# A third plain group becomes a Sevens group in both gated MLPs, and the plain weights' remainders move to accumulating DMAs

## The chip, the cores and the metric

The kernel runs on one core of a Trainium2 chip. Its time is the device time of one execution in microseconds (us). The engines named below are TensorE (PE; PEld is its weight load), VectorE (DVE), ScalarE (ACT), GpSimd (POOL) and SyncE (SP); the last two here mostly issue DMA transfers.

## The reference

A decoder trunk of two layers on 512 tokens of width 1024, all in float32. Layer 0 mixes by attention (8 forgetting heads and 8 stick-breaking heads), layer 1 by a gated short convolution. Each is followed by the gated MLP that this case is about (D_FF = 2816):

```python
def conv_ffn(h, norm_g, w_up, conv_w, w_down):
    xn = rms_norm(h, norm_g)
    u = causal_dwconv(xn @ w_up, conv_w)
    g, val = u[..., :D_FF], u[..., D_FF:]
    return (jax.nn.silu(g) * val) @ w_down

for layer in range(DEPTH):          # DEPTH = 2
    ...                             # h = h + the mixer of this layer
    h = h + conv_ffn(h, ffn_norm[layer], ffn_w_up[layer], ffn_conv[layer], ffn_w_down[layer])
```

## The kernel before

**Float32 on TensorE.** Each float32 operand is split into a rounding ("hi") and a remainder ("lo"), and a product is three matmuls: hi hi, hi lo, lo hi (`mm3`, L283 to L285). For weights, ScalarE writes the rounding `whi` (L262) and VectorE subtracts it from the raw weight to give `wlo` (L263). Weights that a `want` call asks for come in chunks of 128 x 1024 values (512 KB) by SP's queue into a tile `raw`; `fetch` runs AHEAD = 2 chunks before use, and `whi`, `wlo` and `raw` have three buffers each.

**The up projection** of an MLP makes 22 + 22 tiles of 128 columns, in 11 groups of two gate and two value tiles. The first CLASSIC groups are plain: per group 2 pairs x 2 halves x 8 k-tiles x 3 matmuls on 512 tokens. The other groups go by class `Sevens`, a scheme of seven block products instead of eight: p1, p7, p3, p6, p2, q5, q4, each of 24 matmuls on 256 tokens (`seven`, L1010). Its weights come as four 512-KB blocks X, Y, W, Z; Y and X get a second block added by accumulating POOL transfers (`add_block`, L1033), Y also takes X (L1062) and W (L1106) on VectorE. `halves_to` makes their halves (ACT L959, DVE L963 or L965). For p3 the previous group is used, so the first Sevens group ("base group") runs p1, p7, p6, p2, q5, q4.

**Chores.** The VectorE and ScalarE work beside the plain groups is written as generators: `normed` multiplies a PSUM accumulator by the row of the norm (L1201), `prepare` makes the moving operands of the Sevens (L1185, L1192, L963), `gate_one` runs the convolution (L390, L393), SiLU and the product of gate and value (L997, L998). `work_off(us)` lets that much of them be issued per three matmuls (SHARE) or per slot of the base group.

**The down projection** (L1527) is again the seven products, in the order p1, p7, p2, p6, p3, q5, q4, each in six steps of 2, 2, 2, 1, 2, 2 k-tiles. Before a step, `operand` makes the halves of its activations, `sums` updates the blocks of activations (L1428 to L1432), `bring` and the chain transfers (L236, L238) add weight blocks; for three of them a block `other` is loaded and added by VectorE into `Y_chain`, `p1_hi_chain` or `p1_lo_chain` (L233). L1463 adds a finished accumulator to the residual. Layer 0 streams activations of 256 columns, layer 1 streams weights of 512 columns.

**Order.** A tile scheduler orders the instructions of each engine by its own estimate of times. What is passed to `tc.keep_in_program_order` stays in the order in which the program emits it, against other instructions so marked on that engine. The hi parts of the Sevens' weights (L959) and the POOL transfers are so marked.

## Time and profile before

| | us |
|---|---|
| median of 3 runs | 1135.77 (1134.57 to 1136.08) |
| the profiled execution | 1138.21 |
| its span in the trace | 1136.2 |
| TensorE busy in it | 1122.1 |
| plain groups of layer 0 | 278.95 to 346.60 |
| Sevens groups of layer 0 | 346.60 to about 504 |
| down projection of layer 0 | about 504 to 600 |
| plain groups of layer 1 | 793.7 to 861.7 |
| down projection of layer 1 | about 1018 to 1132 |

The profile comes from one execution. Its page gives the busy time of each engine, the chain of work that ended last, the costliest groups of instructions and the DMA issues; further views of the same trace give the waits of an engine, its instructions in order of time, and tables of busy time by stretch. "A <- B: t" in the waits means that A sat idle until B was done. "DMA share" is the mean busy share of the core's 16 DMA engines, and the clock is the one granted to TensorE, 1.00 being full. Line numbers are those of the kernel before.

### The profile page before, as it was taken

The numbers are of one execution on the slowest core, as the hardware profiler recorded it, in microseconds if no ns is written. First come the engines' busy times: TensorE is split into PE (matmuls) and PEld (weight loads), VectorE is DVE, ScalarE is ACT, GpSimd is POOL, SyncE is SP. The second block draws the span as 40 slices with busy tenths as digits, with TensorE's granted clock in tenths as the row PEclk, the third lists the DMA queues.
The fourth block names the chain that finished last, engine by engine and source line by source line (L and its number), as shares of the span: only waits on it lengthen the run. The fifth ranks groups of instructions, "written<-read, shape, count | busy, mean of one in ns | idle before, by whom it ended". The sixth has DMA issues, their size and how long they took to land.

```text
span 1136.2 us, 19079 instructions
## 1 busy us (share of the span) xinstructions
PE 1122.1 (99%) x7547; PEld 1007.1 (89%) x7547; DVE 965.4 (85%) x1459; ACT 670.3 (59%) x999; POOL 133.0 (12%) x150
## 2 busy tenths in 40 slices
PE   8999999999999999999999999999999999999998
PEld 7888787878889999999999889988889999998886
DVE  6787888887899898989878888875798999889886
ACT  7556576755546767676547445544445766667553
POOL 4000000000012111014300001000001211014300
PEclk9999999999999999999999999999999999999999
DMA  6412212022366867689971655633375786789961
GB/s 192 112 38 75 57 39 74 26 87 75 106 182 118 191 160 163 172 235 194 224 185 31 172 118 142 130 111 93 93 195 112 167 191 137 181 220 216 230 168 56
DMA packets 160440, 155.31 MB, mean 137 GB/s; under 512 B 6396, under 2 KB 136492, under 8 KB 160352
## 3 DMA queue, kind: packets, MB, share of 16 engines
q1 hardware_dynamic: 124256, 106.94, 30.6%
q0 software_dynamic: 35936, 47.10, 25.1%
q8 instruction: 59, 0.97, 0.3%
q14 instruction: 29, 0.24, 0.1%
q10 hardware_dynamic: 160, 0.07, 0.0%
HBM read 149.10 MB, written 2.10 MB: 133 GB/s over the span
## 4 chain that ended last, share of the span: by engine, by line
PE 87%; DVE 6%; issue 2%; DMA 2%; ACT 2%; POOL 1%; DVEq 0%; SPq 0%; POOLq 0%; ACTq 0%
PE psb L1010 25%; PE psa L1010 10%; PE psb L1527 9%; PE psb L283 6%; PE psb L284 6%; PE psb L285 6%; PE psa L1527 6%; PE psa L285 4%; PE psa L283 4%; PE psa L284 4%; PE psb L658 1%; PE psa L754 1%; DMA raw<-in_ffn_w_down 1%; DVE rest L699 1%; DVE wlo L263 1%
## 5 line engine op out<-in xcount | busy, mean ns | idle before, releaser
L262 ACT ACTIVATE whi<-raw 128x1024 fp32r<-128x1024 f32 (+2 forms) x97 | 100.1, 1034 | 103.9 <-PE psb L284 31.9
L263 DVE TENSOR_TENSOR wlo<-raw,whi 128x1024 fp32r<-128x1024 f32 (+2 forms) x97 | 115.2, 1188 | 30.5 <-ACT whi L262 29.6
L1010 PE MATMUL psb<-p_hi,wlo_p 128*128 128x256 f32 x384 | 108.3, 282 | 0.6 <-DVE wlo_p L963 0.6
L1010 PE MATMUL psb<-p_lo,whi_p 128*128 128x256 f32 x384 | 108.1, 281 | 0.0
L1010 PE MATMUL psb<-p_hi,whi_p 128*128 128x256 f32 x384 | 107.8, 281 | 0.0
L283 PE MATMUL psb<-hs_a,whi 128*128 128x512 f32 x256 | 104.4, 409 | 0.0
L285 PE MATMUL psb<-hs_a,wlo 128*128 128x512 f32 x256 | 101.5, 397 | 0.0
L1010 PEld LDWEIGHTS psb<-p_hi,wlo_p 128*128 128x128 f32 x384 | 72.2, 188 | 0.8 <-DVE wlo_p L963 0.8
L1010 PEld LDWEIGHTS psb<-p_hi,whi_p 128*128 128x128 f32 x384 | 72.8, 190 | 0.0
L1010 PEld LDWEIGHTS psb<-p_lo,whi_p 128*128 128x128 f32 x384 | 72.3, 188 | 0.0
L1010 PE MATMUL psb<-q_hi,whi_q 128*128 128x256 f32 x256 | 72.0, 281 | 0.0
L1010 PE MATMUL psa<-p_lo,whi_p 128*128 128x256 f32 x256 | 72.0, 281 | 0.0
L1010 PE MATMUL psb<-q_lo,whi_q 128*128 128x256 f32 x256 | 72.0, 281 | 0.0
L1010 PE MATMUL psa<-p_hi,wlo_p 128*128 128x256 f32 x256 | 72.0, 281 | 0.0
L1010 PE MATMUL psb<-q_hi,wlo_q 128*128 128x256 f32 x256 | 72.0, 281 | 0.0
L1010 PE MATMUL psa<-p_hi,whi_p 128*128 128x256 f32 x256 | 71.8, 281 | 0.0
L1527 PE MATMUL psb<-act,whi 128*128 128x256 f32 x352 | 63.1, 282 | 0.0
L393 DVE SCALAR_TENSOR_TENSOR uv<-yv,taps,uv 128x511 f32<-128x511 f32 (+1 forms) x88 | 62.5, 744 | 0.2
L393 DVE SCALAR_TENSOR_TENSOR ug<-yg,taps,ug 128x511 f32<-128x511 f32 (+1 forms) x88 | 61.9, 743 | 0.3 <-ACT ug L390 0.3
L285 PEld LDWEIGHTS psb<-hs_a,wlo 128*128 128x128 f32 x256 | 48.1, 188 | 10.9
L283 PEld LDWEIGHTS psb<-hs_a,whi 128*128 128x128 f32 x256 | 48.4, 189 | 10.5 <-issue 1.2
L1527 PE MATMUL psb<-whi,act 128*128 128x512 f32 x176 | 56.7, 398 | 0.0
(458 smaller groups left out, 3645.7 us busy)
## 6 DMA issues: line engine op xcount, KB each, us to landing
raw<-in_attn_w_in SPq DMA_DIRECT2D x24, 512.0 KB, 4.0
raw<-in_ffn_w_up SPq DMA_DIRECT2D x24, 512.0 KB, 3.9
X<-in_ffn_w_up SPq DMA_DIRECT2D x16, 512.0 KB, 4.7
W<-in_ffn_w_up SPq DMA_DIRECT2D x16, 512.0 KB, 6.7
Y<-in_ffn_w_up SPq DMA_DIRECT2D x16, 512.0 KB, 4.5
Z<-in_ffn_w_up SPq DMA_DIRECT2D x16, 512.0 KB, 4.8
Y<-in_ffn_w_up POOLq DMA_DIRECT2D x16, 512.0 KB, 9.8
X<-in_ffn_w_up POOLq DMA_DIRECT2D x16, 512.0 KB, 7.4
```

The source lines that it names most:

```text
L262: return (act.activation(hi[:, at_], raw[:, at_], AF.Copy), dve.tensor_tensor(lo[:, at_], raw[:, at_], f32(hi[:, at_]), op=ALU.subtract))
L263: dve.tensor_tensor(lo[:, at_], raw[:, at_], f32(hi[:, at_]), op=ALU.subtract))
L283: made = [pe.matmul(acc, w[0], rhs[0], start=first, stop=False), pe.matmul(acc, w[0], rhs[1], start=False, stop=False), pe.matmul(acc, w[1 ...
L284: pe.matmul(acc, w[0], rhs[1], start=False, stop=False),
L285: pe.matmul(acc, w[1], rhs[0], start=False, stop=last)]
L393: dve.scalar_tensor_tensor(dst[:, d:], src[:, 0:S - d], tap(j), dst[:, d:], op0=ALU.mult, op1=ALU.add)
L658: pe.matmul(ss[e][:, c:c + wide], ql[rows, b * P:n], kl[rows, 0:wide], start=first and b == bs[0], stop=last and b == bs[-1])
L699: dve.tensor_tensor_scan(back, back, begin[:, S - n:S][:, ::-1], 0.0, op0=ALU.mult, op1=ALU.max)
L754: pe.matmul(out_, w, t[:, first:first + step * (NB - k - 1) + 1:step, :], start=k == 0 and i == 0, stop=k == NB - 1 and i == 1)
L1010: pe.matmul(to, w[a][:, k, c], x[b][:, k, :], start=fresh and i + k + t == 0, stop=i == 1 and k == 3 and t == 2, skip_group_check=not fresh)
L1527: pe.matmul(to, l, r, start=begin and o + t == 0, stop=end and t == 2 and o == (0 if layer else 1), skip_group_check=not fresh)
```

## The change

1. CLASSIC goes from 3 to 2 and SHARE from 0.58 to 0.68: each MLP has two plain groups and nine Sevens groups.
2. The weight chunks of the plain groups are in a set `by_dma`. For these ScalarE writes the rounding and then the negated rounding into `wlo`, and a POOL transfer adds `raw` to it; VectorE does nothing for them.
3. The accumulators of the second plain group stay in PSUM, and its `normed` and `gate_one` chores run in the slots of the first Sevens groups, at a rate that depends on the group. Their wide tiles lie in the buffer `hs_a`, which held the moving operand of the plain groups.
4. In the base group the halves for p6 are emitted ahead of a ScalarE copy.
5. In the down projections the halves of the activations (from the second phase on), the `sums` and the additions of `bring` are marked to keep the program's order.
6. The first weight chunk of the kernel is loaded in two halves.

```diff
@@ -46,8 +46,8 @@
 NSUMS, NROWS, LATE = 4.0, 3.0, 7.0
 FILL1, FILL2, BEFORE = 1.5, 3.3, 2.0
 UNITS = (0, 1), (2,), (3,)
-CLASSIC = 3
-SHARE = 0.58
+CLASSIC = 2
+SHARE = 0.68
 
 
 @with_exitstack
@@ -217,7 +217,7 @@
 
         wanted.append((place, nk, n, blocks, queue))
 
-    brought = {}
+    brought, pin = {}, tc.keep_in_program_order
 
     def bring(i):
         place, nk, n, blocks, queue = wanted[i]
@@ -230,7 +230,7 @@
             if queue is dve:
                 other = wp.tile([P, CHUNK], F32, tag="raw", name=f"other{i}")
                 nc.sync.dma_start(other[:, 0:nk * n].rearrange("p (k c) -> p k c", c=n), src)
-                dve.tensor_tensor(raw[:, 0:nk * n], raw[:, 0:nk * n], other[:, 0:nk * n], op=ALU.add)
+                pin(dve.tensor_tensor(raw[:, 0:nk * n], raw[:, 0:nk * n], other[:, 0:nk * n], op=ALU.add))
             elif not fresh or queue:
                 tc.keep_in_program_order(
                     nc.gpsimd.dma_start(v, src, **({} if fresh else {"accum_op": ALU.add})))
@@ -251,14 +251,21 @@
             raw = wp.tile([P, CHUNK], F32, tag="raw", name=f"raw{i}")
             v = raw[:, 0:nk * n].rearrange("p (k c) -> p k c", c=n)
             to = 0
+            step = nk // 2 if i == 0 else nk
             for c0, width in zip(parts[::2], parts[1::2]):
-                with nc.allow_non_contiguous_dma(reason="eight columns"):
-                    nc.sync.dma_start(
-                        v[:, :, to:to + width], dram[k0 * P:(k0 + nk) * P, c0:c0 + width].rearrange("(k p) c -> p k c", p=P))
+                for k in range(0, nk, step):
+                    with nc.allow_non_contiguous_dma(reason="eight columns"):
+                        nc.sync.dma_start(
+                            v[:, k:k + step, to:to + width],
+                            dram[(k0 + k) * P:(k0 + k + step) * P, c0:c0 + width].rearrange("(k p) c -> p k c", p=P))
                 to += width
 
         def part(a, b):
             at_ = slice(a * n, b * n)
+            if i in by_dma:
+                act.activation(hi[:, at_], raw[:, at_], AF.Copy)
+                act.activation(lo[:, at_], raw[:, at_], AF.Copy, scale=-1.0)
+                return pin(nc.gpsimd.dma_start(lo[:, at_], raw[:, at_], accum_op=ALU.add))
             return (act.activation(hi[:, at_], raw[:, at_], AF.Copy),
                     dve.tensor_tensor(lo[:, at_], raw[:, at_], f32(hi[:, at_]), op=ALU.subtract))
         halve[i] = part, nk
@@ -424,7 +431,10 @@
     want_out(0)
     want_out_last()
 
+    by_dma = set()
+
     def want_ffn(layer, pairs=NF):
+        by_dma.update(range(len(wanted), len(wanted) + 2 * pairs))
         for j in range(pairs):
             want(ffn_w_up[layer], 0, 8, j * P, P)
             want(ffn_w_up[layer], 0, 8, DFF + j * P, P)
@@ -955,14 +965,15 @@
 
     work_scope.close()
 
-    def halves_to(hi, lo, src, sign=1.0, held=False):
+    def halves_to(hi, lo, src, sign=1.0, held=()):
         made = act.activation(hi, src, AF.Copy, scale=sign)
-        if held:
-            tc.keep_in_program_order(made)
         if sign > 0:
-            dve.tensor_tensor(lo, src, f32(hi), op=ALU.subtract)
+            rest = dve.tensor_tensor(lo, src, f32(hi), op=ALU.subtract)
         else:
-            dve.scalar_tensor_tensor(lo, src, -1.0, f32(hi), op0=ALU.mult, op1=ALU.subtract)
+            rest = dve.scalar_tensor_tensor(lo, src, -1.0, f32(hi), op0=ALU.mult, op1=ALU.subtract)
+        for m, engine in ((made, "act"), (rest, "dve")):
+            if engine in held:
+                pin(m)
 
     LEFT, RIGHT = slice(0, HT), slice(HT, S)
     FORMS = ("p1", "p7", "p3", "p6", "p2", "q5", "q4")
@@ -1035,7 +1046,7 @@
         def weights_of(self, g, form, n):
             hi, lo = (wp.tile([P, CHUNK], F32R, tag=f"w{t}", name=f"w{t}_{form}{self.name}{g}", bufs=3)[:, 0:1024].rearrange(
                 "p (k c) -> p k c", c=2 * P) for t in ("hi", "lo"))
-            halves_to(hi, lo, self.st[g][n], held=True)
+            halves_to(hi, lo, self.st[g][n], held=("act",))
             self.st[g][form] = hi, lo
 
         def bank_of(self, g, n):
@@ -1074,8 +1085,8 @@
         def slot(self, g, s):
 
             on, was, soon = (i in self.groups for i in (g, g - 1, g + 1))
-            if g == self.groups[0]:
-                self.work_off(1.4 if s < 4 else 1e9)
+            if self.chores:
+                self.work_off(self.rate(g, s))
             form, n, fresh = (("p1", "A", True), ("p7", "T", True), ("p3", "R", False), ("p6", "R", False), ("p2", "A", False),
                               ("q5", "R", False), ("q4", "T", False))[s]
             if s == 2:
@@ -1094,8 +1105,11 @@
                 if soon:
                     self.load_pair(g + 1)
             elif s == 1:
+                if on and not was:
+                    self.weights_of(g, "p6", "Y")
                 if on:
                     act.activation(self.bank_of(g, "R"), c["A"], AF.Copy, scale=-1.0)
+                if on and was:
                     self.weights_of(g, "p6", "Y")
                 if soon:
                     self.add_block(g + 1, "Y", 1, 1)
@@ -1132,6 +1146,9 @@
 
         chores, credit, ahead = (), 0.0, False
 
+        def rate(self, g, s):
+            return 1.4 if s < 4 else 1e9
+
         def work_off(self, us):
             if self.norm.row is None:
                 return
@@ -1154,7 +1171,13 @@
 
         up = Sevens(layer, mp, range(CLASSIC, HF), block_of)
         up.norm, up.chores = norm, []
-        up.wides_of = lambda g: {n: mp.tile([P, 2, S], F32, tag=n, name=f"{n}{layer}{g}", bufs=1) for n in ("yg", "yv", "ug", "uv")}
+
+        def wides_of(g):
+            if g == CLASSIC - 1:
+                t = hsp.tile([P, 8, S], F32, tag="hs_a", name=f"hs_a_wide{layer}")
+                return {n: t[:, 2 * i:2 * i + 2, :] for i, n in enumerate(("yg", "yv", "ug", "uv"))}
+            return {n: mp.tile([P, 2, S], F32, tag=n, name=f"{n}{layer}{g}", bufs=1) for n in ("yg", "yv", "ug", "uv")}
+        up.wides_of = wides_of
         wides, forms, chores = up.wides, up.forms, up.chores
 
         def taps_of(g, half, i):
@@ -1175,6 +1198,7 @@
             elif s == 5:
                 blocks.product(2 * p, 2, wides[p]["ug"], wides[p]["uv"])
         up.tail = tail
+        up.rate = lambda g, s: 1.3 if g == base else 1.0 if g == base + 1 and s < 2 else 0.5
 
         def prepare(half):
             k0 = 2 * half
@@ -1210,10 +1234,11 @@
             blocks.product(2 * g + i, 1, u[0][:, i:i + 1, :], u[1][:, i:i + 1, :])
             yield 0.86
 
+        kept = []
         for j in range(2 * CLASSIC):
             accs = []
             for half in range(2):
-                accs.append(bank("ab"[half]))
+                accs.append(bank(("ab", "ab", "bb", "cc")[j][half]))
                 for _ in products(accs[-1], weights()):
                     up.work_off(SHARE)
                 if j == 2 * CLASSIC - 1 and half == 1:
@@ -1222,11 +1247,10 @@
             if j == 2 * CLASSIC - 2:
                 up.load_pair(base)
                 up.add_block(base, "Y", 1, 1)
-            chores.append(normed(j // 2, j % 2, accs))
-            if j in (0, 2):
-                chores.append(prepare(j // 2))
-            for i in {1: (0, 1), 3: (2, 3), 4: (4,), 5: (5,)}.get(j, ()):
-                chores.append(gate_one(i // 2, i % 2))
+            kept.append(accs)
+            if j < 2:
+                chores.extend((normed(0, j, accs), prepare(j)))
+        chores.extend([gate_one(0, i) for i in range(2)] + [normed(1, i, kept[2 + i]) for i in range(2)] + [gate_one(1, i) for i in range(2)])
         slots = [(lambda g=g, s=s: up.slot(g, s)) for g in range(CLASSIC, HF + 1) for s in range(7)]
         return blocks, slots
 
@@ -1416,7 +1440,7 @@
             k0, nk = GROUPS[g]
             name, sign = SOURCE[PHASES[p]]
             t = acts[i] = mp.tile([P, 2, 2, HT], F32R, tag=act_tags[i % 4], name=f"act{layer}_{i}")
-            halves_to(t[:, 0, 0:nk, :], t[:, 1, 0:nk, :], blocks.block(name, k0, nk), sign)
+            halves_to(t[:, 0, 0:nk, :], t[:, 1, 0:nk, :], blocks.block(name, k0, nk), sign, held=("act", "dve") if p else ())
 
         def sums(i):
             if i >= len(steps):
@@ -1425,11 +1449,11 @@
             if p in (1, 2, 3):
                 a, b, c, d = (blocks.block(n, *GROUPS[g]) for n in "abcd")
                 if p == 1:
-                    dve.tensor_tensor(b, b, c, op=ALU.add)
+                    pin(dve.tensor_tensor(b, b, c, op=ALU.add))
                 elif p == 2:
-                    dve.tensor_tensor(a, b, a, op=ALU.subtract)
+                    pin(dve.tensor_tensor(a, b, a, op=ALU.subtract))
                 else:
-                    dve.tensor_tensor(b, b, d, op=ALU.add)
+                    pin(dve.tensor_tensor(b, b, d, op=ALU.add))
 
         n_up = 7 * (HF - CLASSIC)
         for i, fn in enumerate(slots[:n_up]):
```

**VectorE in the plain stage and at the base group.** Before, near the end of the plain stage of layer 0, from the last but one of its weight remainders (`wlo` at L263) to the last:

```order
L263 TENSOR_TENSOR wlo_3736<-raw_3737,whi_3735 128x1024
L1192 TENSOR_TENSOR Y_prep_3705<-Y_prep_3705,px_prep_3704 128x2x256
L963 TENSOR_TENSOR q_lo_3377<-Y_prep_3705,q_hi_3376 128x512
L963 TENSOR_TENSOR q_lo_3379<-px_prep_3704,q_hi_3378 128x512
L963 TENSOR_TENSOR p_lo_3373<-Y_prep_3705,p_hi_3372 128x512
L1201 TENSOR_TENSOR yg_3684<-psa_3649,nrow_n_3489 128x512
L1192 TENSOR_TENSOR Y_prep_3705<-px_prep_3704,Y_prep_3705 128x2x256
L1201 TENSOR_TENSOR yv_3685<-psb_3693,nrow_n_3489 128x512
L263 TENSOR_TENSOR wlo_3779<-raw_3780,whi_3778 128x1024
```

After, the same engine from the first write into `hs_a_wide` (the second plain group's normalised tiles) to the remainder for p2, which is split from W:

```order
L1225 TENSOR_TENSOR hs_a_wide_3825<-psb_3575,nrow_n_3495 128x512
L971 TENSOR_TENSOR wlo_p_3805<-Y_3664,whi_p_3804 128x1024
L1008 TENSOR_TENSOR head_3368<-ug_3504,uv_3505 128x256
L1120 TENSOR_TENSOR Y_3664<-Y_3664,W_3773 128x1024
L1009 SCALAR_TENSOR_TENSOR head_3368<-ug_3504,uv_3505 128x256
L1225 TENSOR_TENSOR hs_a_wide_3825<-psb_3620,nrow_n_3495 128x512
L1225 TENSOR_TENSOR hs_a_wide_3825<-psc_3668,nrow_n_3495 128x512
L1225 TENSOR_TENSOR hs_a_wide_3825<-psc_3701,nrow_n_3495 128x512
L400 SCALAR_TENSOR_TENSOR hs_a_wide_3825<-hs_a_wide_3825,taps 128x511 x2
L400 SCALAR_TENSOR_TENSOR hs_a_wide_3825<-hs_a_wide_3825,taps 128x510
L971 TENSOR_TENSOR wlo_p_3817<-W_3773,whi_p_3816 128x1024
```

The remainders of the plain chunks are gone from VectorE, and the normalisations of the last plain group have moved behind the first remainders of the base group.

**POOL at the same place.** After, the last two of the eight accumulating transfers of plain weights in layer 0 (L268) and what stands behind them on POOL:

```order
L268 DMA wlo_3577<-raw_3578 128x1024
L268 DMA wlo_3622<-raw_3623 128x1024
L1044 DMA Y_3664<-in_ffn_w_up 128x4x256
L1044 DMA X_3663<-in_ffn_w_up 128x4x256
L1044 DMA Y_3776<-in_ffn_w_up 128x4x256
```

The accumulations into Y and X of the base group, the first transfers of the MLP on this queue before, now stand behind the eight new ones.

**VectorE in the down projection of layer 0, near its fifth product.** Before (L263 is the remainder of a weight, L965 that of an activation, L233 the addition in `bring`):

```order
L263 TENSOR_TENSOR wlo_6661<-raw_6662,whi_6660 128x512
L965 SCALAR_TENSOR_TENSOR act_28_6724<-hs_b_blocks_4316,act_28_6724 128x512
L233 TENSOR_TENSOR Y_chain_0_5850<-Y_chain_0_5850,other_6847 128x512
L263 TENSOR_TENSOR wlo_6695<-raw_6696,whi_6694 128x1024
L965 SCALAR_TENSOR_TENSOR act_29_6745<-hs_b_blocks_4316,act_29_6745 128x512
L263 TENSOR_TENSOR wlo_6728<-raw_6729,whi_6727 128x1024
```

After (the same remainders are at L270 and L973, and act_28 is the same step):

```order
L270 TENSOR_TENSOR wlo_6790<-raw_6791,whi_6789 128x1024
L973 SCALAR_TENSOR_TENSOR act_28_6819<-hs_b_blocks_4411,act_28_6819 128x512
L270 TENSOR_TENSOR wlo_6823<-raw_6824,whi_6822 128x1024
L973 SCALAR_TENSOR_TENSOR act_29_6840<-hs_b_blocks_4411,act_29_6840 128x512
L270 TENSOR_TENSOR wlo_6844<-X_chain_0_5861,whi_6843 128x1024
L973 SCALAR_TENSOR_TENSOR act_30_6872<-head_3368,act_30_6872 128x512
L270 TENSOR_TENSOR wlo_6876<-X_chain_0_5895,whi_6875 128x1024
L973 SCALAR_TENSOR_TENSOR act_31_6904<-head_3368,act_31_6904 128x512
L1487 TENSOR_TENSOR h<-h,psa_6718 128x2x256
L233 TENSOR_TENSOR Y_chain_0_5945<-Y_chain_0_5945,other_6942 128x512
```

The addition into `Y_chain` stood one operand behind the remainder of the step before; it now stands behind four more remainders.

## The prediction

> **What bounds the kernel now.** The page comes first: the share of each engine, and the chain that ended last.
>
> ```profile
> PE 1122.1 (99%) x7547; PEld 1007.1 (89%) x7547; DVE 965.4 (85%) x1459; ACT 670.3 (59%) x999; POOL 133.0 (12%) x150
> PE 87%; DVE 6%; issue 2%; DMA 2%; ACT 2%; POOL 1%; DVEq 0%; SPq 0%; POOLq 0%; ACTq 0%
> ```
>
> TensorE is busy in 1122.1 of 1136.2 us, so only two things can change the time much: fewer or shorter matmuls, and the 14.1 us in which TensorE is idle (or the places where its clock drops). Next, therefore, what TensorE waits for (us in total, times, longest), the rows that the change touches:
>
> ```profile
> PE psa L1527 <- DVE wlo L263: 2.3, 2, 2.1
> PE psa L283 <- ACT whi L262: 1.3, 1, 1.3
> PE psb L1527 <- DVE wlo L263: 0.8, 1, 0.8
> PE psb L1010 <- DVE wlo_p L963: 0.6, 1, 0.6
> ```
>
> L1527 is the down projection: three waits for a weight remainder from VectorE, 3.1 us, of which one is 2.1. L1010 is a product of the Sevens, 0.6 us. Third, the table by stage (stretch, its us, then busy us and instructions of PE, PEld, DVE, ACT, POOL, then granted clock, DMA share, GB/s):
>
> ```profile
> 278.95:346.60 67.65, 67.65 (x299) 54.94 (x297) 62.36 (x102) 34.84 (x49) 3.80 (x3) 1.00 0.47 125
> 364.00:384.00 20.00, 20.00 (x171) 20.00 (x171) 18.43 (x24) 13.36 (x17) 4.35 (x4) 1.00 0.80 182
> 530.00:550.00 20.00, 19.24 (x162) 19.04 (x161) 18.36 (x27) 9.03 (x13) 9.09 (x9) 1.00 0.90 177
> 570.00:590.00 20.00, 17.86 (x138) 17.66 (x137) 13.22 (x17) 9.06 (x13) 0.00 (x0) 0.91 0.78 211
> 590.00:610.00 20.00, 20.00 (x171) 20.00 (x170) 16.56 (x22) 11.41 (x17) 0.00 (x0) 1.00 0.20 56
> 1040.00:1080.00 40.00, 40.00 (x190) 32.40 (x189) 36.95 (x53) 24.38 (x37) 16.20 (x16) 1.00 1.02 215
> ```
>
> The first row is the plain groups of layer 0, the second a Sevens group, the next three the down projection of layer 0, the last that of layer 1. TensorE is full in the groups, but VectorE is at 92% there (62.36 of 67.65, 18.43 of 20), so it has little room. One stretch stands out: 138 matmuls in 570 to 590 against 171 in the next 20 us, at a clock of 0.91.
>
> **Part 1: one more Sevens group for a plain one, in each MLP.** A plain group is 2 x 2 x 8 x 3 = 96 matmuls of 512 columns; a Sevens group is 7 x 24 = 168 of 256 columns. Their price is the distance between starts (start us, us, what, from the chain):
>
> ```profile
> 316.93 0.23 PE psa L284
> ...
> 329.54 0.23 PE psa L284
> ...
> 376.03 2.84 PE psa L1010 x24
> ```
>
> L284 is every third matmul; from 316.93 to 329.54 lie 18 steps of three, 12.61 / 54 = 0.2335 us a matmul, and a plain group takes 96 x 0.2335 = 22.4. A product takes 2.84, a Sevens group 7 x 2.84 = 19.9. The exchange gives 2.5 us per MLP, 5.1 us in both. This is work of the engine that sets the end, so it is gained in full if the added group is fed as the others are: its blocks come by the same loads as those of 364 to 384, where TensorE had no gap at DMA share 0.80. VectorE gains 12 remainders (part 2) and takes on one Sevens group instead of a plain one; that is below, under the base group.
>
> **Part 2: the plain weights' remainders by accumulating DMA.** The 8 chunks of 512 KB of each MLP's two plain groups now take two ScalarE passes and one POOL transfer from SBUF to SBUF; VectorE loses its subtraction. Rows of the page (the first two, and the last: the median over the whole span), and between them of the DMA issues in 282 to 350:
>
> ```profile
> L262 ACT ACTIVATE whi<-raw 128x1024 fp32r<-128x1024 f32 (+2 forms) x97 | 100.1, 1034 | 103.9 <-PE psb L284 31.9
> L263 DVE TENSOR_TENSOR wlo<-raw,whi 128x1024 fp32r<-128x1024 f32 (+2 forms) x97 | 115.2, 1188 | 30.5 <-ACT whi L262 29.6
> ...
> Y<-in_ffn_w_up POOLq DMA_DIRECT2D x2, 512.0 KB, 8.3
> head<-head POOLq DMA_DIRECT2D x2, 256.0 KB, 4.1
> ...
> X<-in_ffn_w_up POOLq DMA_DIRECT2D x1, 512.0 KB, 7.2
> ...
> Y<-in_ffn_w_up POOLq DMA_DIRECT2D x16, 512.0 KB, 9.8
> ```
>
> Twelve subtractions of 1.19 us (8 changed, 4 of the third group gone) are 14.3 us less on VectorE per MLP. ScalarE gains 8 x 1.03 = 8.3 us; it is 35 of 67.65 busy there, which covers that. The new cost is delay: no row before shows 512 KB accumulated from SBUF. The nearest are 4.1 us for 256 KB in SBUF and 7.2 to 8.3 for 512 KB accumulated from DRAM, so I take 4.1 as the lower bound, 8.3 as the upper, and 7 as likely. A chunk's chain is then 2 x 1.03 + 7 = 9.1 us (6.2 to 10.4). It starts when the three-deep buffer is free, two chunks ahead of use: a chunk is 24 matmuls, 24 x 0.2335 = 5.6 us, so the chain has 11.2 us. It fits at both bounds, with 0.8 to 5 us to spare, hence no cost; without that cover each chunk beyond would cost a third of the excess, since three chunks are in flight.
>
> The Trainium skill, "SBUF — State Buffer", section "SBUF: two separate sides", speaks against this part: a VectorE operation that holds the port pair shared with GpSimd keeps GpSimd from writing the descriptors of its DMAs. [...]
>
> **Part 3: the base group.** The first Sevens group now starts after two thirds of the plain stage, at 278.95 + 45.1 = 324.0. In its slots VectorE must also do the second plain group's normalisations and convolutions, into the buffer of the moving operand, whose first write waits until the last plain matmul has read it. By the order of VectorE's instructions these stand behind that wait and ahead of the remainder for the product p2: four normalisations, the sum of Y and W, the remainder for p6, two small products and three convolutions. Rows of 316 to 364 (busy us, mean ns):
>
> ```profile
> L393 DVE SCALAR_TENSOR_TENSOR uv<-yv,taps,uv 128x510 f32<-128x510 f32 (+1 forms) x9 | 6.7, 743 | 0.0
> ...
> L1201 DVE TENSOR_TENSOR yg<-psa,nrow_n 128x512 f32<-128x512 f32 x4 | 2.7, 684 | 0.5 <-PE psa L285 0.5
> ...
> L997 DVE TENSOR_TENSOR head<-ug,uv 128x256 f32<-128x256 f32 x5 | 2.1, 417 | 0.1
> ...
> L1106 DVE TENSOR_TENSOR Y<-Y,W 128x1024 f32<-128x1024 f32 x1 | 1.2, 1219 | 0.0
> ```
>
> Starts lie about 0.08 us closer than these durations (part 4 shows 0.61 for 0.69, 1.14 for 1.22). So 4 x 0.60 + 3 x 1.14 (with p2's own remainder) + 2 x 0.34 + 3 x 0.66 = 8.5 us: ready at 332.5. TensorE wants it after p1, p7 and p6, 324.0 + 3 x 2.84 = 332.5. There is no slack at all. I charge 0.5 us for each MLP, 1.0 in all, with bounds 0 and 2 (one such operation more ahead). What waits behind a late remainder is TensorE itself. The 0.6 of wait at L1010 goes: p6's remainder now is the second instruction behind that wait, some 1.8 us after 324.0 against a need at 329.7. This needs the sum Y that it splits in time, and its POOL transfers stand behind the eight new ones. The last of these is issued about when its chunk's buffer is free and ScalarE is through: 324.0 - 5.6 - 11.2 + 2.1 = 309, and 8.3 us more leave Y in place before 324.
>
> **Part 4: the pinned down projection.** VectorE and ScalarE about the large wait (start us, us, what), the chain, and TensorE around it:
>
> ```profile
> 577.03 5.10 DMA other<-in_ffn_w_down
> ...
> 576.31 0.69 DVE L263 TENSOR_TENSOR wlo<-raw,whi 128x512 fp32r<-128x512 f32 x1 [1.98 <-ACT whi L262]
> 576.92 0.69 DVE L965 SCALAR_TENSOR_TENSOR act<-hs_b_blocks,act 128x512 fp32r<-128x512 f32 x1
> 582.15 0.69 DVE L233 TENSOR_TENSOR Y_chain<-Y_chain,other 128x512 f32<-128x512 f32 x1 [4.55 <-DMA other<-in_ffn_w_down]
> 582.76 1.22 DVE L263 TENSOR_TENSOR wlo<-raw,whi 128x1024 fp32r<-128x1024 f32 x1
> 583.90 0.68 DVE L965 SCALAR_TENSOR_TENSOR act<-hs_b_blocks,act 128x512 fp32r<-128x512 f32 x1
> ...
> 579.26 1.06 ACT L262 ACTIVATE whi<-raw 128x1024 fp32r<-128x1024 f32 x1 [2.46 <-DMA raw<-in_ffn_w_down]
> ...
> 581.60:584.04 2.44, 0.30 (x4) 0.10 (x2) 1.89 (x3) 2.44 (x4) 0.00 (x0) 1.00 0.06 9
> 584.04:588.20 4.16, 4.16 (x22) 4.16 (x23) 4.16 (x6) 0.60 (x2) 0.00 (x0) 0.59 0.87 268
> 588.20:591.00 2.80, 2.80 (x26) 2.80 (x26) 2.55 (x3) 1.58 (x2) 0.00 (x0) 1.00 0.68 191
> ```
>
> The remainder at 582.76 could have started at 580.3, when its rounding was done, but the addition into Y_chain stood ahead of it and waited 4.55 us for a transfer. TensorE ran dry, then ran at clock 0.59 for 4.16 us. The row 570 to 590 gives the whole loss: 171 - 138 = 33 matmuls of 0.118, 3.9 us; idle and slow clock together (2.14 + 4.16 x 0.41 = 3.9) agree. In the new order the addition stands behind the remainders of the next four steps, so it waits alone and the 3.9 us go. What is late next is the addition's own reader, which comes four rows behind it, two remainders and an operand later.
>
> The Trainium skill, "TensorE: Matmul & The Clock Gate", section "What's actually happening", has the clock halved only after an idle window of about 3.4 us. The trace differs: 2.44 us sufficed. By the rule the gap alone would count, and this term would be 2.1 instead of 3.9.
>
> The other two waits, 0.8 at 534 and 0.2 at 553, come from sums bunched ahead of a remainder:
>
> ```profile
> 530.75 1.02 DVE L1428 TENSOR_TENSOR head<-head,hs_a_blocks 128x512 f32<-128x512 f32 x2
> 531.69 0.68 DVE L1428 TENSOR_TENSOR hs_b_blocks<-hs_b_blocks,hs_a_blocks 128x512 f32<-128x512 f32 x1
> 532.29 0.68 DVE L1430 TENSOR_TENSOR head<-head 128x512 f32<-128x512 f32 x1
> 532.89 1.22 DVE L263 TENSOR_TENSOR wlo<-q_hi_chain,whi 128x1024 fp32r<-128x1024 f32 x1
> ```
>
> Four sums lay ahead; pinned, one does. Both waits go, 1.0 us. Layer 1's down projection already runs with DMA share 1.02 and VectorE at 92% without a gap, so its pins cost nothing and gain nothing.
>
> **Part 5: the first attention chunk in two loads.** The 1.3 us wait at L283 is TensorE's start, behind one load in the chain:
>
> ```profile
> 1.23 5.18 DMA raw<-in_attn_w_in
> ```
>
> Two halves may let ScalarE begin up to 0.35 us earlier and delay the loads of x by an issue, 0.5: from -0.35 to +0.5, I take 0.
>
> **Sum.** 5.1 + 3.9 + 1.0 + 0.6 - 1.0 = 9.6 us. The profiled execution took 1138.21 (span 1136.2 and 2.0 around it), 2.4 above the median of 1135.77; the difference is taken off the median: **1126.2 us**.
>
> **Rivals.** *One: the down projection's stall moves.* Its transfers keep the DMA engines at a share of 0.90 in 530 to 550. If a weight load lands late rather than an order being wrong, TensorE waits at another step and the clock drops again. For: the 577.03 transfer took 5.1 us. Against: layer 1. Gain 5.1 + 0.6 - 1.0 = 4.7: 1131.
>
> *Two: the base group starves.* If VectorE is later than counted by 2 us or more at p2, clock loss follows as at 584, about 4 us in each MLP: 9.6 + 1.0 - 8 = 2.6 gained, 1133. For: no slack, VectorE 92% busy. Against: 14.3 us of subtractions gone.
>
> *Three: the accumulating transfers are late (slower).* If the chain of a chunk takes C over 11.2 us, the plain stages lose (C - 11.2) / 3 for each of 16 chunks. All of the 9.6 is gone at C = 13; at C = 16 the loss is 25.6, the time 1152. For: over the whole span the median Y accumulate took 9.8 us, which with 2.1 of ScalarE is already 11.9. Against: the stage's DMA share is 0.47, and there the accumulates took 7.2 to 8.3.
>
> *Four: nothing changes* (within 2.3 us), if the plain matmul's price holds for the added products too: the 2.84 of a product speaks against it.
>
> **How the numbers follow.** Forecast 0.58, rival one 0.16, two 0.13, three 0.10, four 0.03. A measurement of this kernel tells 0.2%, 2.3 us, from no change. Faster: 0.58 + 0.16 and most of rival two, 0.82; same: the rest of two and four, 0.07; slower: rival three, 0.11. The likeliest case alone gives 1124.5 (no new stalls, a better start) to 1129 (both bounds bad). The range takes in rivals one and two, 1122 to 1133, since either sign of the small terms is open by about 2 us below; rival three is left out.
>
> **What would show it.** Right: the plain stages 22.4 us shorter and one more stretch of 19.9; no wait of L1527's line on a remainder above 0.3 us in layer 0, and clock 1.00 all through 560 to 600; no wait of TensorE on a plain remainder. Wrong: waits of TensorE on the plain remainders with the POOL transfers above 9 us (rival three), waits in the base group near 332 and 847 with a lower clock after them (two), or a new wait in 504 to 600 on a rounding whose load is late (one).

## The result, and the profile after

The changed kernel took 1160.96 us (median of 4 runs, 1159.27 to 1161.43) against 1135.92 us before: a ratio of 1.0213, 95% interval 1.0200 to 1.0226. The forecast was 1126.2, the range 1122 to 1133. The change is slower by 25 us. (The two profiled executions, on which the views below rest, took 1159.27 and 1138.21: 21 us apart.)

The page of the changed kernel, then TensorE's waits in it (us in total, times, longest):

```profile
span 1157.5 us, 19436 instructions
PE 1129.8 (98%) x7691; PEld 1017.2 (88%) x7691; DVE 959.5 (83%) x1445; ACT 690.9 (60%) x1029; POOL 151.8 (13%) x170
...
PE psa L1021 <- DVE wlo_p L971: 3.7, 12, 1.0
PE psb L1021 <- ACT Xs L1069: 3.6, 2, 1.9
PE psa L1021 <- ACT whi_p L969: 3.0, 2, 2.0
PE psa L1551 <- DVE wlo L270: 1.8, 2, 0.9
```

L1021 is the product of the Sevens now, L1551 the down projection. The waits of the Sevens have grown from 0.6 to more than 10 us, those of the down projection have fallen from 3.1 to 1.8. TensorE's busy time has grown by 7.7 us although its work is 5 us less. Some 5 of these 12.7 us are a lower clock: the rows below with 0.81, 0.93 and 0.63, and 676 to 686 with 0.83, lose 6.7 us, against 1.8 before in 570 to 590. The rest fits the way in which a wait is counted, as seen at one of them: at the wait of 0.21 us that ends at 945.68, the next two matmuls start after 0.48 and 0.22 us instead of 0.12 each, so the wait costs 0.46 us, of which 0.21 count as idle (this was not added up over all waits). By stage (stretch, its us, busy us and instructions of PE, PEld, DVE, ACT, POOL, granted clock, DMA share, GB/s):

```profile
326.00:334.00 8.00, 6.24 (x40) 5.83 (x39) 4.21 (x6) 2.64 (x3) 0.99 (x2) 0.81 0.13 22
334.00:342.00 8.00, 5.25 (x36) 4.57 (x35) 8.00 (x13) 4.79 (x7) 2.80 (x3) 0.93 1.03 157
342.00:350.00 8.00, 7.28 (x42) 7.25 (x42) 6.19 (x9) 4.23 (x7) 0.00 (x0) 0.63 0.71 203
500.00:520.00 20.00, 16.99 (x139) 16.38 (x138) 15.99 (x20) 14.30 (x20) 3.06 (x3) 1.00 0.97 257
520.00:600.00 80.00, 80.00 (x678) 80.00 (x677) 71.90 (x98) 47.85 (x66) 24.24 (x22) 1.00 0.98 219
```

The last row is most of the down projection of layer 0: full, at clock 1.00, where 570 to 590 had shown 0.91. The first three are the base group: in 24 us 118 matmuls, where some 200 fit. The fourth is the last Sevens group of layer 0.

A ledger makes this exact. Its borders are the first and last starts of TensorE's groups (first product p1, first matmul of a down projection, last matmul of the attention and so on); us of each stage:

| stage | before | after | expected by the prediction |
|---|---|---|---|
| to the last attention matmul | 277.6 | 278.9 | 277.6 |
| to the first Sevens product of layer 0 | 69.0 | 46.9 | 46.6 |
| Sevens of layer 0 | 157.3 | 192.5 | 177.2 |
| down projection of layer 0 | 118.6 | 113.8 | 113.7 |
| to the first product of the convolution's Sevens | 46.3 | 47.1 | 46.3 |
| from there to its last p2 | 71.0 | 74.9 | 71.0 |
| output projection of layer 1's mixer | 52.9 | 52.9 | 52.9 |
| plain groups and Sevens of layer 1 | 225.6 | 230.9 | 223.1 |
| down projection of layer 1 | 113.8 | 115.1 | 113.8 |

(In the column of expectations a Sevens group is 19.9 and a plain group 22.4, and the prediction's allowance of 0.5 for each base group and its gain of 0.6 at L1010 are left out. By this ledger the down projection of layer 0 ends at 622.5 before, not at about 600 as the table of times before has it.) The losses against the prediction are 15.3 us in the Sevens of layer 0, 7.8 in layer 1, 3.9 and 0.8 in the convolution, 1.3 at the start and 1.3 at the end.

**The base group.** What VectorE did around its start, and the queue of SyncE and POOL before it (start us, us, engine, line, operation; idle time before it in brackets):

```profile
320.10 1.23 DVE L971 TENSOR_TENSOR wlo_p<-X,whi_p 128x1024 fp32r<-128x1024 f32 x1
329.76 1.22 DVE L971 TENSOR_TENSOR wlo_p<-Y,whi_p 128x1024 fp32r<-128x1024 f32 x1 [8.43 <-ACT whi_p L969]
...
328.67 1.06 ACT L969 ACTIVATE whi_p<-Y 128x1024 fp32r<-128x1024 f32 x1 [8.85 <-DMA Y<-in_ffn_w_up]
...
305.60 0.37 SPq L1041 DMA_DIRECT2D W<-in_ffn_w_up  x1
306.06 0.46 SPq L1036 DMA_DIRECT2D X<-in_ffn_w_up  x1
314.94 0.37 SPq L1041 DMA_DIRECT2D Z<-in_ffn_w_up  x1
315.40 0.51 SPq L1037 DMA_DIRECT2D Y<-in_ffn_w_up  x1
...
305.86 0.86 POOL L268 DMA_DIRECT2D wlo<-raw  x1 [5.01 <-ACT wlo L267]
311.20 0.85 POOL L268 DMA_DIRECT2D wlo<-raw  x1 [4.48 <-ACT wlo L267]
320.93 1.32 POOL L1044 DMA_DIRECT2D Y<-in_ffn_w_up  x1 [8.88 <-DMA Y<-in_ffn_w_up]
```

Read from the bottom: the accumulation into Y was issued at 320.93, since the load of Y had been issued only at 315.40. That load stood on SyncE's queue behind the load of Z, which needs one of the three weight buffers; the transfer of 305.86 held that buffer until 314.9. So Y's rounding ran at 328.67, and VectorE, whose next instruction was Y's remainder, sat idle for 8.43 us with all the work of the base group queued behind. From 330 to 346 it ran without a pause, and TensorE waited four times in this stretch.

**Every Sevens group.** In the last group of layer 0, as in 16 of the 18 groups, VectorE's instructions now stand otherwise than before (three lines of before, then the same three after):

```profile
484.59 0.68 DVE L1053 TENSOR_TENSOR yg<-psb,Xs 128x512 f32<-128x512 f32 x1
485.19 1.21 DVE L963 TENSOR_TENSOR wlo_p<-Z,whi_p 128x1024 fp32r<-128x1024 f32 x1
486.32 2.73 DVE L393 SCALAR_TENSOR_TENSOR ug<-yg,taps,ug 128x511 f32<-128x511 f32 x4
...
498.74 1.22 DVE L971 TENSOR_TENSOR wlo_p<-Z,whi_p 128x1024 fp32r<-128x1024 f32 x1
499.87 0.68 DVE L1064 TENSOR_TENSOR yg<-psb,Xs 128x512 f32<-128x512 f32 x1
501.41 1.54 DVE L400 SCALAR_TENSOR_TENSOR ug<-yg,taps,ug 128x511 f32<-128x511 f32 x2 [0.85 <-ACT ug L397]
```

The subtraction that joins yg (the join, from here on) stands behind the remainder for p3, which is split from Z; before, it stood ahead of it, in all 16 groups. ScalarE makes ug from yg, and VectorE's next instruction needs ug: it idles 0.85 us. Over the whole kernel this is a row of its own in VectorE's waits:

```profile
DVE wlo_p L971 <- ACT whi_p L969: 15.2, 4, 8.4
...
DVE ug L400 <- ACT ug L397: 12.7, 15, 0.9
```

The experiments ask which of these orders costs what, and whether the parts of the change do what was predicted once they are mended.

### The profile page after: what moved, and what is told of

It reads as the page before. It is cut to its first block, busy times and chain, and to the rows that moved or that the text cites. A ratio compares the mean times of both kernels' runs of the same rounds, so it can differ in the third digit from the quotient of the medians.

```text
span 1157.5 us, 19436 instructions
## 1 busy us (share of the span) xinstructions
PE 1129.8 (98%) x7691; PEld 1017.2 (88%) x7691; DVE 959.5 (83%) x1445; ACT 690.9 (60%) x1029; POOL 151.8 (13%) x170
## 5 line engine op out<-in xcount | busy, mean ns | idle before, releaser
L1021 PE MATMUL psb<-p_hi,whi_p 128*128 128x256 f32 x432 | 122.3, 283 | 1.8 <-ACT whi_p L969 1.0
L1021 PE MATMUL psb<-p_hi,wlo_p 128*128 128x256 f32 x432 | 122.4, 283 | 0.8 <-DVE wlo_p L971 0.8
L1021 PE MATMUL psb<-p_lo,whi_p 128*128 128x256 f32 x432 | 122.3, 283 | 0.0
L269 ACT ACTIVATE whi<-raw 128x1024 fp32r<-128x1024 f32 (+2 forms) x73 | 74.7, 1026 | 70.6 <-PE psa L291 17.2
L270 DVE TENSOR_TENSOR wlo<-raw,whi 128x1024 fp32r<-128x1024 f32 (+2 forms) x73 | 86.0, 1179 | 19.5 <-ACT whi L269 19.0
L292 PE MATMUL psb<-hs_a,wlo 128*128 128x512 f32 x224 | 88.7, 397 | 0.0
L1021 PE MATMUL psa<-p_hi,wlo_p 128*128 128x256 f32 x288 | 84.3, 293 | 3.7 <-DVE wlo_p L971 3.7
L1021 PE MATMUL psa<-p_hi,whi_p 128*128 128x256 f32 x288 | 82.2, 286 | 3.0 <-ACT whi_p L969 3.0
L1021 PE MATMUL psb<-q_hi,whi_q 128*128 128x256 f32 x288 | 81.6, 283 | 3.6 <-ACT Xs L1069 3.6
L1021 PEld LDWEIGHTS psb<-p_hi,whi_p 128*128 128x128 f32 x432 | 82.6, 191 | 2.2 <-ACT whi_p L969 1.2
L1021 PEld LDWEIGHTS psb<-p_hi,wlo_p 128*128 128x128 f32 x432 | 81.9, 190 | 1.0 <-DVE wlo_p L971 1.0
L1021 PEld LDWEIGHTS psb<-p_lo,whi_p 128*128 128x128 f32 x432 | 82.1, 190 | 0.0
L1021 PE MATMUL psa<-p_lo,whi_p 128*128 128x256 f32 x288 | 82.0, 285 | 0.0
L1021 PE MATMUL psb<-q_lo,whi_q 128*128 128x256 f32 x288 | 81.2, 282 | 0.0
L1021 PE MATMUL psb<-q_hi,wlo_q 128*128 128x256 f32 x288 | 81.0, 281 | 0.0
L400 DVE SCALAR_TENSOR_TENSOR ug<-yg,taps,ug 128x511 f32<-128x511 f32 (+1 forms) x80 | 59.5, 749 | 13.2 <-ACT ug L397 12.7
L400 DVE SCALAR_TENSOR_TENSOR uv<-yv,taps,uv 128x511 f32<-128x511 f32 x80 | 59.7, 749 | 6.4 <-ACT uv L397 5.4
L1551 PE MATMUL psb<-act,whi 128*128 128x256 f32 x352 | 63.0, 282 | 0.1
L1021 PEld LDWEIGHTS psa<-p_hi,wlo_p 128*128 128x128 f32 x288 | 55.2, 192 | 7.2 <-DVE wlo_p L971 6.8
L1021 PEld LDWEIGHTS psa<-p_hi,whi_p 128*128 128x128 f32 x288 | 55.6, 193 | 3.5 <-ACT whi_p L969 3.5
L1021 PEld LDWEIGHTS psb<-q_hi,whi_q 128*128 128x128 f32 x288 | 54.7, 190 | 4.2 <-ACT Xs L1069 4.0
```

The source lines that it names most:

```text
L269: return (act.activation(hi[:, at_], raw[:, at_], AF.Copy), dve.tensor_tensor(lo[:, at_], raw[:, at_], f32(hi[:, at_]), op=ALU.subtract))
L270: dve.tensor_tensor(lo[:, at_], raw[:, at_], f32(hi[:, at_]), op=ALU.subtract))
L292: pe.matmul(acc, w[1], rhs[0], start=False, stop=last)]
L400: dve.scalar_tensor_tensor(dst[:, d:], src[:, 0:S - d], tap(j), dst[:, d:], op0=ALU.mult, op1=ALU.add)
L1021: pe.matmul(to, w[a][:, k, c], x[b][:, k, :], start=fresh and i + k + t == 0, stop=i == 1 and k == 3 and t == 2, skip_group_check=not fresh)
L1551: pe.matmul(to, l, r, start=begin and o + t == 0, stop=end and t == 2 and o == (0 if layer else 1), skip_group_check=not fresh)
```

## Experiments

The runs of one group shared their runs of the kernel before; its median lay between 1135.7 and 1136.8, so kernels of different groups are compared by their ratios to it.

**1. The base group's loads first.** On SyncE's queue Y of the base group is pinned ahead of W and Z; every other engine has the same instructions in the same order.

```diff
-            nc.sync.dma_start(s["X"], self.block_of(g, 0, 0))
-            nc.sync.dma_start(s["Y"], self.block_of(g, 0, 1))
+            for n, half in (("X", 0), ("Y", 1)):
+                made = nc.sync.dma_start(s[n], self.block_of(g, 0, half))
+                if n in "Y" and g == CLASSIC and self.name != "c":
+                    pin(made)
...
+            if n in ('W', 'Z') and g == CLASSIC and self.name != "c":
+                pin(made)
```

> The changed kernel with one thing moved: on SyncE's queue the load of block Y of the first Sevens group stands ahead of the loads of W and Z (in the changed kernel Y stood behind Z in layer 0 and behind W in layer 1, and these waited for a weight buffer that an accumulating DMA held). The instructions of all other engines stay in the same order. Theory one (the queue: late Y empties VectorE for 8.4 us in layer 0 and 4.7 in layer 1): Y is issued near 307.6, no wait of TensorE in 326 to 346, clock 1.00 there; about 9 us of the loss in layer 0 and 2 to 3 in layer 1 come back, time 1147 to 1151. Theory two (the second plain group's chores are too much work for VectorE in the base group): VectorE stays full behind the base group, TensorE waits as before, 1158 to 1161.

Measured: 1150.2 us (1146.88 to 1152.83), ratio 1.0122 (1.0095 to 1.0150), some 10 us less than the change's 1.0213. SyncE, and the base group:

```profile
309.18 0.37 SPq L1037 DMA_DIRECT2D Y<-in_ffn_w_up  x1
309.64 1.27 SPq L1043 DMA_DIRECT2D W<-in_ffn_w_up  x1
...
322.17 0.46 SPq L1043 DMA_DIRECT2D Z<-in_ffn_w_up  x1
...
326.00:334.00 8.00, 8.00 (x64) 7.77 (x63) 7.96 (x13) 3.85 (x6) 3.79 (x3) 1.00 0.93 194
334.00:342.00 8.00, 7.21 (x61) 7.00 (x60) 8.00 (x12) 6.35 (x9) 0.00 (x0) 1.00 0.86 193
342.00:350.00 8.00, 8.00 (x70) 8.00 (x69) 7.80 (x11) 4.36 (x6) 2.61 (x2) 1.00 0.31 88
```

Y is issued 6 us earlier, and in the same 24 us TensorE does 195 matmuls at clock 1.00. What is left is one wait of 0.80 us on p2's remainder: the step that the prediction had priced at 0.5. The second plain group's chores are thus not too much for VectorE; the queue was the cause here. The Sevens of layer 0 still take 184.6, and layer 1 stays at 229.8.

**2. VectorE's subtraction again** (`by_dma.update(())` in the changed kernel).

> The changed kernel with VectorE's subtraction again for the remainders of the plain weights; all else as changed. Theory one: weight buffers come free some 6 us earlier, W and Z are loaded earlier, Y is no longer held up, the base groups lose little; VectorE has 9.5 us more work per MLP in the plain stage: 1147 to 1153. Theory two: VectorE has still more to do, 1163 or more.

Measured: 1145.88 us, ratio 1.0088 (1.0072 to 1.0104). With the buffers freed by VectorE, Z is loaded at 305.90 and Y at 312.45, and TensorE has no wait in the base group of layer 0. Taking the accumulating DMAs out gains some 14 us, a little more than the first theory's range, and still leaves 10. The buffers are not the only reason: in this run the scheduler also left the join ahead in eight of the nine groups of layer 1 (in the changed kernel in one), and layer 1 takes 225.5 us instead of 230.9.

**3. The pins alone**, in the kernel before (part 5 of the change).

> The kernel before with the pinned down projection alone. The prediction's step (3.9 + 1.0 us in layer 0, nothing in layer 1): 1131 (1130 to 1132), no wait on a weight remainder in the down projection of layer 0. Rival: the stall moves to another step, 1134 to 1136.

Measured: 1134.07 us, ratio 0.9976 (0.9966 to 0.9986). The down projection of layer 0 takes 113.3 instead of 118.6, a little more than predicted, and no wait of its line is left. The convolution behind it takes 0.9 more, a wait on the remainder for its p6. The gain on the whole is 2 to 4 us, below the 4.9 of the prediction. The time is the one that the rival named, but the stall did not move within the down projection.

**4. The accumulating DMAs alone**, in the kernel before, on all 12 plain chunks.

> The kernel before with the accumulating DMAs alone, on all 12 plain chunks of each MLP. Theory one: the loads of the base group are again held up by weight buffers that the DMAs hold, unless Y stands ahead of them; if it does not, 1140 to 1148. Theory two: VectorE is relieved of 28 us and nothing is lost, 1133 to 1136.

Measured: 1139.23 us, ratio 1.0028 (1.0016 to 1.0040). Neither number was hit. Here Y happens to stand ahead of W and Z (Y at 318.96, Z at 335.18), and the base groups lose only 0.42 and 1.54 us in layer 0 and 1.09 in layer 1. On the whole, relieving VectorE gained nothing in the kernel before.

**5 to 8. Three more edits**, on top of the first. SHARE also paces the chores of the convolution's input projection; with 0.68 three splits of activations are emitted ahead of the weights of p1 there. The edits:

```diff
# 5: in the convolution's input projection
-                up.work_off(SHARE)
+                up.work_off(0.58)
# 6: the first chunk in one load
-            step = nk // 2 if i == 0 else nk
+            step = nk
# 7: slot 0 of the Sevens
+                    self.join(p, "yg", st[p]["T"], st[p]["Xs"])
                     if "p3" not in st[p]:
                         self.weights_of(p, "p3", "Z")
-                    self.join(p, "yg", st[p]["T"], st[p]["Xs"])
```

> The kernel of the run with the base loads first, and the chores of layer 1's convolution (its input projection also uses SHARE) at 0.58 per three matmuls again, as before the change. With it ScalarE's rounding for the first product p1 of that stage stands ahead of the last three splits of activations again. Theory (SHARE reached a stage that the change did not mean): from the first p1 product of the convolution to its last p2 71 to 72 us instead of 75.3, no wait at 679; 3 to 4 us less than the base-loads run, about 1146.5. Rival (these us come from the shifted start of that stage): no change.

Measured: 1145.26 us, ratio 1.0082 (1.0067 to 1.0097); the stage takes 72.1 instead of 75.3. The wait at 679 is gone; one of 0.9 on p6 stays, which run 3 showed with the pins alone.

> The kernel of the run with the base loads first, with the first weight chunk in one load again. Theory (the second load delays the loads of x): the attention's last output matmul at 277.6 instead of 280.4 or 278.9, no wait on x_tok above 0.2; 1 to 2.5 us less than the base-loads run. Rival (the halves help or do nothing): same or slower.

Measured: 1149.0 us, ratio 1.0117 (1.0100 to 1.0134), against 1.0122 (1.0095 to 1.0150): not told apart. In the profile the attention ends at 277.7 and the wait on x_tok is gone, but the six profiled runs with the halves ended it at 278.1 to 280.4 and the four with one load at 277.6 to 278.1, so about 1 us at most hangs on this edit.

> The kernel of the run with the base loads first; in each Sevens slot the subtraction that joins the last accumulator (yg) is emitted ahead of the halves for p3, so that VectorE does it first, as in the kernel before (in the changed kernel the scheduler put it behind in nearly all groups). Theory three (an order locked a little late: VectorE idles 0.85 us per group behind the join, p2's remainder is 0.2 late in each group and the last groups end late): the waits of 0.2 per group go, those of 1.8 and 1.7 on q5 shrink, 4 to 9 us less than the base-loads run, 1141 to 1146. Rival (VectorE has simply no time to catch up): waits stay, 1149 to 1151.

Measured: 1133.48 us, ratio 0.9981 (0.9967 to 0.9996): 16 us less, far more than expected, and 2 us faster than the kernel before. (With the join ahead, the scheduler placed other instructions of each group as before, too.) TensorE's waits in the Sevens of both MLPs shrink to one row, and the row of VectorE waiting for ug is gone:

```profile
PE psa L1021 <- DVE wlo_p L971: 0.9, 2, 0.7
```

The Sevens of layer 0 take 177.1 us and the span of layer 1 223.4: the 177.2 and 223.1 of the prediction's own price.

> The three edits of the other runs of this call together, with the base loads first. If they add up: 1134 to 1140. If the loss behind the base group is VectorE's work and not its order: 1143 to 1147.

Measured: 1129.53 us (1129.32 to 1130.99), ratio 0.9946 (0.9932 to 0.9961). It is below the range for edits that add up; the ratios do add up, nearly. This beats the kernel before by 6 us and, by the ratios, the change by 30.

**9. The join alone**: edit 7 on the changed kernel, with the base loads as the change has them.

> The changed kernel with the join of yg emitted ahead of the halves for p3, and nothing else: SyncE's queue has Y behind Z and W as in the changed kernel. It parts the two causes. If the late Y costs its 9 us in layer 0 and 2 to 3 in layer 1 by itself: 1142 to 1146, with TensorE's waits in the first base group as in the changed kernel. If the order of the join was the whole cause and the late Y is caught up later: 1133 to 1136.

Measured: 1146.83 us, ratio 1.0097 (1.0080 to 1.0114). This is just above the first range. The Sevens of layer 0 take 186.0, and TensorE waits in the base group again. In layer 0 the two orders cost about the same, and each by itself: against 177.2, the late Y alone leaves 8.8 us (run 9), the late join alone 7.4 (run 1), both 15.3 (the change), neither -0.1 (run 7). In layer 1, against 223.1, these are 3.0, 6.7, 7.8 and 0.3: there the two do not add up.

**10. All but the accumulating DMAs**: run 8 with VectorE's subtraction.

> The kernel with all three edits and the base loads first, with VectorE's subtraction for the plain remainders instead of the accumulating DMAs. Theory (the DMAs relieve VectorE by 9.5 us per MLP, which the base groups need): TensorE waits 1 to 3 us more in each base group, 1132 to 1136. Rival (the DMAs gain nothing once the orders are mended): 1128 to 1131.

Measured: 1135.35 us, ratio 0.9995 (0.9985 to 1.0004), against 0.9946 of run 8. With the orders mended, the accumulating DMAs are worth 0.5%, 5 to 6 us; the loss without them is mostly in the Sevens of layer 0, 181.5 against 177.9. The time is the theory's, the place is not: TensorE does not wait in either base group, but later in layer 0, 0.58 us at 365.09 and 1.94 at 378.48, with a lower clock behind the second (0.73 in 380 to 384).

**11. p2's halves one slot earlier** in the base groups, on run 8 (`weights_of(g, "p2", "W")` in slot 1 instead of slot 2).

> The kernel with all three edits and the base loads first, and in the base groups the halves of p2's weights emitted one slot earlier, so that they no longer stand behind the copy of P7s on ScalarE and the second plain group's normalisations on VectorE. Theory (the waits of 1.0 in each base group, which the prediction put at 0.5, are of this order): both go, 1126.5 to 1128.5. Rival (VectorE is full there, the wait moves to q5 or q4): 1129 to 1131.

Measured: 1129.61 us, ratio 0.9939 (0.9924 to 0.9953). The waits on p2's remainder, 1.00 and 0.98 us in run 8, are gone from the profile and have not moved to q5 (0.2). The time is the same within the intervals: inconclusive about a gain of up to 2 us.

**12. The late join in the kernel before**, to see whether this order does the damage with no base group in trouble (the edit without the small changes to the helpers that it needs):

```diff
-                        self.weights_of(p, "p3", "Z")
-                    self.join(p, "yg", st[p]["T"], st[p]["Xs"])
+                        self.weights_of(p, "p3", "Z", True)   # its remainder pinned
+                    m = self.join(p, "yg", st[p]["T"], st[p]["Xs"])
+                    if self.name != "c":
+                        tc.keep_in_program_order(m)
```

> The kernel before with the one order put in that the changed kernel had: in every Sevens slot the join of yg pinned behind the remainder for p3 on VectorE. Theory three (this order alone makes VectorE late in every Sevens group, whatever the base group does): waits of about 0.2 per group on p2's remainder and 1.7 to 1.9 on q5 in the last group of each MLP, 5 to 14 us slower, 1142 to 1151. Rival (the order hurts only behind a base group that starts late): 1136 to 1138.

Measured: 1148.05 us, ratio 1.0095 (1.0076 to 1.0113). TensorE's waits in this kernel, then VectorE's:

```profile
PE psb L1010 <- ACT Xs L1060: 5.7, 3, 3.2
PE psa L1531 <- DVE wlo L263: 3.6, 3, 1.8
PE psa L1010 <- DVE wlo_p L963: 1.4, 7, 0.2
...
DVE ug L393 <- ACT ug L390: 12.2, 15, 0.9
```

It is the signature of the changed kernel: 0.2 us in a group on p2, 1.9 us on q5 in the last group of layer 0 (at 503.39; in the changed kernel 1.88 at 512.49), 0.9 at the start of the down projection, and the same row of 15 waits of up to 0.9 us. (On q5 in the last group of layer 1 it is 3.2, against 1.7 in the changed kernel.) The edit fixes the order of two instructions in each of the 16 groups. The scheduler then also moved others of VectorE and ScalarE, to where the changed kernel has them: two of the convolutions of ug, for instance, now stand behind the remainder for p6. This order as a whole costs some 11 us by the ratio (9 to 13), with the loads and the transfers in the order of before. What the two instructions cost without the others was not tried.

How 0.85 us of idle time can become a wait of 1.9 in the last group is seen at the X block (two lines of before, then the changed kernel):

```profile
483.45 1.23 DVE L1062 TENSOR_TENSOR Y<-Y,X 128x1024 f32<-128x1024 f32 x1
485.21 1.28 POOL L1033 DMA_DIRECT2D X<-in_ffn_w_up  x1 [17.28 <-ACT whi_p L959]
...
497.60 1.23 DVE L1073 TENSOR_TENSOR Y<-Y,X 128x1024 f32<-128x1024 f32 x1
...
499.35 1.28 POOL L1044 DMA_DIRECT2D X<-in_ffn_w_up  x1 [17.80 <-ACT psb L1111]
...
509.33 1.06 ACT L969 ACTIVATE whi_q<-X 128x1024 fp32r<-128x1024 f32 x1 [4.25 <-DMA X<-in_ffn_w_up]
...
511.86 0.58 ACT L1069 ACTIVATE Xs<-psb 128x512 f32<-128x512 f32 x1
```

The accumulation into X comes only after the sum on VectorE has read it; both times it is issued 0.5 us after the sum's end. Counted from the copy of P7s, which follows TensorE, that sum came 6.7 us ahead before (483.45 against 490.11) and 5.2 ahead now (497.60 against 502.84). The transfer takes 9.9 us there (before, 9.6). ScalarE's rounding of X waits for it, and behind this rounding on ScalarE stands the copy Xs, which TensorE waits for at 512.49.

## Why the prediction was wrong, point by point

**Part 1 (5.1 us).** The price was right: with the orders mended the stages take 177.1 and 223.4 us against 177.2 and 223.1. The condition was not met. "Gained in full if the added group is fed as the others are": the others were no longer fed as before, because VectorE's order had changed in 16 of the 18 groups. The prediction read that order at the base group and in the down projection, not in the groups between, which it took to repeat. VectorE was 92% busy there (18.43 of 20 us before), which left little room for another 0.85 us of idle time in a group. Cost: 7.4 us in layer 0 and, by run 1 (229.8 against 223.1), 6.7 in layer 1. This is the larger failure, and no rival named it.

**Part 2 (no cost).** Right in its own terms: the transfers landed in 4.6 to 9.0 us, 5.8 in the median, where 4.1 to 8.3 with 7 as likely was assumed, and TensorE did not wait for a plain remainder that came by DMA. The slowest, 9.0 us, landed at 314.89, just as the matmuls that use it began: with the 2.1 of ScalarE its chain is 11.1 of the 11.2 us that there were. VectorE is busy in 34.5 of 47 us beside them (279 to 326); how much of the 4.6 to 9.0 us is a delay by it, no run here separates. It missed that the transfer holds the raw weight's buffer as long, and who wants that buffer next.

**Part 3 (-1.0).** This step fell: "8.3 us more leave Y in place before 324" counted the POOL queue and its transfers, and took the load of Y for granted. On SyncE's queue that load stood behind W and Z, which wait for the buffers of part 2. Y was in place at 328.6. Cost: 8.8 us in layer 0 and 3.0 in layer 1 (run 9, 226.1 against 223.1), with a lower clock in layer 0. Rival two named the place and the sign, VectorE late at p2, with 4 us per MLP, but another cause, too much work; run 1 shows that the work fits, with waits of 0.80 and 0.82 us for the 0.5 that was charged.

**Part 4 (4.9).** Right in the trace: the down projection of layer 0 is 4.8 us shorter, and its clock is 1.00 throughout. The sign "no wait above 0.3 us" was missed once, by 0.93 us at its start (519.58); that wait is the join's, for it is in runs 1 and 12 and gone in runs 7 and 9. But the term was mis-sized for the median. Of the 3.9 us, 1.7 were a lower clock in the one execution that was profiled, whose mean clock is 0.998; of the 46 executions of the kernel before beside the experiments, 23 have a mean clock of 1.00 and a median of 1135.7 us, and 14 have 0.998 and 1137.9. So part of the 3.9 was not in the median that the gain was taken off, which fits the 2 to 4 us of run 3. The pins are not free elsewhere: run 3 has 0.9 us more in the convolution. In layer 1 the down projection is 1.3 longer in the change, and 0.3 with the join mended.

**Part 5 (0).** Mis-sized at most by 1.3 us; run 6 could not settle it.

**Not in the prediction at all**: SHARE is also used by the convolution's input projection, 3.9 us in the change, of which run 5 gets 3.2 back by undoing it there.

**Rival three** had the sign and not the cause. By its formula a loss of 34.8 us against the forecast needs a chain C of 17.7 us; the longest was 11.1, and the accumulating DMAs were late for nobody on their own path. That the change came out slower, as this rival said, is chance.

With the four edits (run 8) the change gains 6 us where 9.6 were predicted; most of the rest is the base groups' waits of 2.3 for 1.0, 1.1 in the convolution and 0.5 at the start. What made the scheduler swap the join stays open. Neither the pins alone (run 3) nor the accumulating DMAs alone (run 4) do it: there the join stands ahead in all 16 groups. Without the accumulating DMAs (run 2) it is behind in 8 of 18. The moved chores and the new SHARE were not tried by themselves.

## What to carry to other kernels

A transfer that replaces an engine's work holds its source buffer until it lands: look up who takes that buffer next, and what stands behind that load on its queue. When work is moved and a scheduler orders the rest, compare the order in every repeated group, not only where the work was moved; with an engine at 92%, one swap in every group, with what the scheduler moved along with it, cost some 11 us. A pacing constant that two stages share is a change to both.

## What the runs showed of the hardware

An accumulation of 512 KB from SBUF to SBUF landed in 4.6 to 9.0 us, with 0.85 to 0.95 us of POOL each; those from DRAM into Y and X took 1.3 to 1.9 us of POOL.

TensorE's clock does not follow the length of a single gap. In the changed kernel gaps of 1.00 and 0.76 us within 1.3 us were followed by a clock of 0.62 (330 to 334, the first row), while gaps of 1.05 and 0.98 us within 1.6 us in the base group of layer 1 left it at 1.00 (the second and third):

```profile
330.00:334.00 4.00, 3.24 (x16) 3.04 (x16) 3.96 (x6) 1.31 (x2) 0.99 (x2) 0.62 0.00 0
...
861.00:865.00 4.00, 2.03 (x15) 1.59 (x14) 4.00 (x7) 3.73 (x6) 0.00 (x0) 1.00 1.23 194
865.00:869.00 4.00, 3.94 (x33) 3.94 (x34) 4.00 (x7) 2.37 (x4) 0.00 (x0) 1.00 0.96 221
```

Other runs show the same: a gap of 1.94 us was followed by a lower clock in run 10, one of 3.19 us that ends at 1021.85 in run 12 was not (1.00 from 1019 to 1027).

The Trainium skill, "TensorE: Matmul & The Clock Gate", section "What's actually happening", says that the window in which activity is counted runs freely; that one pair of gaps lowers the clock and another of the same size does not agrees with it, while its idle window of about 3.4 us is longer than any of these gaps.
